# Gate logits of two branches by Strassen's method in a hybrid decoder layer

## The chip, the cores and the metric

The kernel runs on one core of a Trainium2 chip. The metric is the device time of one execution in microseconds, as the median of several runs.

## What is computed

One layer on 1024 tokens of width 1024, all in float32. `x` is multiplied by one wide input projection; three causal token mixers (stick-breaking attention, a gated linear recurrence with 64-wide state (HGRN2), and one with low-rank forget gates (GLA)) give three branches of width 256. Each branch n is projected up to 1024 columns and weighted by a gate of its own, whose logits are 1024 more columns of the input projection:

```python
up = jnp.einsum('nbtw,nwd->nbtd', branches, w_up)
gates = jax.nn.sigmoid(jnp.stack([gate_logits_a, gate_logits_b, gate_logits_c], axis=0))
merged = jnp.sum(gates * up, axis=0)
out = jnp.einsum('btd,de->bte', merged, w_out)
return layer_norm(DEEPNORM_ALPHA * x + out, ln_g, ln_b)
```

The gate logits of one branch are thus a product of a 1024 x 1024 matrix of weights and the transposed x (1024 x 1024).

## The kernel before, in words

**Numbers.** Every float32 operand of a matmul is split into a hi part (rounded, by a ScalarE cast, L98) and a lo part (what is left, by a VectorE subtraction, L99; both in `split`). A product is three matmuls: hi x hi, hi x lo, lo x hi. The transposed x stays in on-chip memory as hi and lo: `xh[th][g]` and `xl[th][g]`, where th is the half of the tokens (512) and g the half of the contraction (four k tiles of 128 rows): eight buffers of the tag `x`.

**Weights.** `load_w` (L167) brings 128 columns of weights in pieces of 256 KB into raw buffers (tag `wr`, four of them, issued by SyncE) and splits them into `wh` and `wl` (five buffers each) at a high priority (`at_priority(PW)`).

**Buffers.** The row buffers (`R`, tag `row`, eight of 128x512), the larger ones (`S`, tag `s`, six of 128x1024), `H` (29 of 128x512), `GT` (two) and the PSUM banks (`pmm` three, `pz` two, `ptr` two, `pav` one) are shared by name: whoever asks for one waits until one is released.

**Order.** The mixers are chains (`c_sb`, `c_rec`) whose steps are interleaved in the code with a stream of projection work, a list of generators (L787 to L792) that give way after every six matmuls of 512 columns or so; `advance` takes the next step of the stream, and entries of `later` are run a counted number of steps on. Once the chains are done, the rest of the stream follows alone: what is left of the gates of branch 0 (`g0`), the finish of branch 1's mixer (`f_finish`), then the gates of branch 2 (`g2`) and branch 1 (`g1`). The instructions of each engine are laid in an order at build time, by priority and by what is ready, and an engine then runs its own list in that order.

**A gate block** (`f_gate`, L488). For each of the eight blocks dd of 128 columns: the weights of the logits (eight k tiles, two loads) and of the up projection (two k tiles, one load) are loaded and split; then for each half of the tokens 24 matmuls of 512 columns (`proj_T`, L207) into a PSUM bank, a sigmoid (L499, ScalarE), six up matmuls (L505) into another bank, the product of the two (L510, VectorE) and an addition to the merged row `mT[dd][th]` (L511, GpSimd).

**The tail** (L855 on). `wout` loads and splits the eight blocks of `w_out`, two of them (`NWO`) ahead of the last gate block into H buffers, the other six into the `x` buffers as these come free. For each quarter of the tokens `mT` is split into `mh` and `ml` (eight row buffers in all); for each 128 tokens 48 matmuls of 512 columns (L879) are followed by the layer norm on VectorE (L881 to L894) in a row `xr` (an S buffer, loaded at L870), which goes out through two DMA queues.

Of the kernel before, what the change touches and what calls it, by code (L numbers as in the profile page):

```python
# [7 lines left out]
F32 = mybir.dt.float32  # L8
F32R = mybir.dt.float32r
# [3 lines left out]
ALU = mybir.AluOpType  # L13
# [17 lines left out]
NGT = 2  # L31
PW = -3000000
PX = -3000000
NWO = 2
NWARM = 10
SB_T = 1.6
CV_T = 10.0
# [18 lines left out]
def hybrid_layer_kernel(ctx, tc, x, x_t, w_in, gla_gate_w2, gla_gate_b, hgrn_lb_logits,  # L56
# [12 lines left out]
    def nm(s):  # L69
        cnt[0] += 1  # L70
        return f"{s}_{cnt[0]}"

    def S(name, dt=F32, shape=None):
        return sp.tile(shape or [P, 1024], dt, tag="s", name=nm(name), bufs=NS)

    def H(name, dt=F32, shape=None):
        return sp.tile(shape or [P, 512], dt, tag="h", name=nm(name), bufs=NH)

    def R(name, dt=F32, shape=None):
        return sp.tile(shape or [P, 512], dt, tag="row", name=nm(name), bufs=NROW)  # L80
# [4 lines left out]
    def pmm(shape=None):  # L85
        return ps.tile(shape or [P, 512], F32, tag="mm", name=nm("mm"), bufs=3)

    def pz(shape=None):
        return ps.tile(shape or [P, 512], F32, tag="z", name=nm("z"), bufs=2)
# [7 lines left out]
    def split(hi, lo, src):  # L97
        nc.scalar.copy(hi, src)  # L98
        nc.vector.tensor_tensor(lo, src, hi.bitcast(F32), op=ALU.subtract)  # L99
# [341 lines left out]
    def f_finish(c0, gain, key, out_key):  # L441

        ws = load_w(W, c0)
        while key not in d:
            yield 0.0
        og, yT = d[key], [[H("yT") for _ in range(2)] for _ in range(2)]

        def transposed(tq):
            for c in range(2):
                pt = ptr([P, 4, P])  # L450
                for t4 in range(4):
                    for o, n, c1 in og(tq * 4 + t4):
                        if c1 <= c * P < c1 + n:
                            nc.tensor.transpose(pt[:, t4, :], o[:, c * P - c1:c * P - c1 + P], ident)
                nc.scalar.copy(yT[c][tq], pt.rearrange("p a b -> p (a b)"))

        for tt in range(8):
            pt = yield from proj_N(ws, tt)
            g = GT("gg")[:, 0:256]
            nc.scalar.activation(g, pt, AF.Sigmoid)  # L460
            nc.vector.tensor_tensor(g, pt, g, op=ALU.mult)
            nc.gpsimd.tensor_tensor(g, g, gain, op=ALU.mult)
            for o, n, c in og(tt):
                nc.vector.tensor_tensor(o, o, g[:, c:c + n], op=ALU.mult)
            yield 1.3
            if tt == 3 + FIN:
                transposed(0)
                yield 0.9

        def rest():  # L470
            transposed(1)
            d[out_key] = yT

        later.append([FIN2, rest])

    def f_split(n):
        while ("y", n) not in d:
            yield 0.0
        r = []
        for c in range(2):  # L480
            yh, yl = [H("yh", F32R) for _ in range(2)], [H("yl", F32R) for _ in range(2)]
            for th in range(2):
                split(yh[th], yl[th], d["y", n][c][th])
            r.append((yh, yl))
        d["ys", n] = r
        yield 0.0

    def f_gate(n, first, d0=0, d1=8):  # L488
        for dd in range(d0, d1):
            if first:  # L490
                d.setdefault("mT", []).append([H("mT") for _ in range(2)])
            ug = load_w(W, GATE0 + 1024 * n + dd * P, P)
            uu = load_w(w_up[0, n], dd * P, P)
            for th in range(2):
                mT = d["mT"][dd][th]
                pt = yield from proj_T(ug, th)
                yield 1.3
                gt = GT("gt")
                nc.scalar.activation(gt, pt, AF.Sigmoid)  # L499
                pu = pmm()  # L500
                k = 0
                for c in range(2):
                    (wh, wl), (a, b) = uu[c], d["ys", n][c]
                    for w_, y_ in ((wh, a), (wh, b), (wl, a)):
                        mm(pu, w_, y_[th], start=(k == 0), stop=(k == 5))  # L505
                        k += 1
                if first:
                    nc.vector.tensor_tensor(mT, pu, gt, op=ALU.mult)  # L508
                else:
                    nc.vector.tensor_tensor(gt, pu, gt, op=ALU.mult)  # L510
                    nc.gpsimd.tensor_tensor(mT, mT, gt, op=ALU.add)  # L511
                yield 1.3

    woh, wol = [], []

    def wout(ks):
        for k in ks:
            if k < NWO:
                wh, wl = [[H("wo", F32R) for _ in range(2)] for _ in range(2)]
            else:  # L520
                w = xp.tile([P, 4, 512], F32R, tag="x", name=nm("wo"))
                wh, wl = [[w[:, 2 * i + e] for e in range(2)] for i in range(2)]
            for e in range(2):
                raw = wp.tile([P, 512], F32, tag="wr", name=nm("wr"), bufs=NWR)
                nc.sync.dma_start(raw, w_out[0, k * P:(k + 1) * P, half[e]])
                with at_priority(PW):
                    split(wh[e], wl[e], raw)
            woh.append(wh)
            wol.append(wl)

    def f_wout(ks):
        wout(ks)
        yield 0.0
# [98 lines left out]
    def c_rec(key, nh, V):  # L632
# [139 lines left out]
        for i, o in enumerate(og):  # L772
# [15 lines left out]
              ("fC", f_cv()), (("ag", 1), f_ag(1)), ("KC", f_ck()), ("GLA", f_cq()),  # L788
              (("ys", 0), f_split(0)), ("g0", f_gate(0, True, 0, 2)), ("vH", f_hi()), (("H", 0), f_h(0)),
              (("y", 2), f_finish(C_G, gng, "ogC", ("y", 2))), (("H", 1), f_h(1)), ("g0", f_gate(0, True, 2, 8)),  # L790
              (("y", 1), f_finish(H_G, hng, "ogH", ("y", 1))), (("ys", 2), f_split(2)), ("g2", f_gate(2, False)),
              (("ys", 1), f_split(1)), ("g1", f_gate(1, False, 0, 7)), ("wo", f_wout(range(NWO))), ("g1", f_gate(1, False, 7, 8))]  # L792
    pos = [0]
    later = []
    budget = [0.0]
# [1 line left out]
    def advance():  # L797

        while pos[0] < len(stream):
            for entry in list(later):  # L800
                entry[0] -= 1
                if entry[0] < 0:
                    later.remove(entry)
                    entry[1]()
            try:
                return next(stream[pos[0]][1])
            except StopIteration:
                done.add(stream[pos[0]][0])
                pos[0] += 1
        return None  # L810
# [26 lines left out]
    for label, mk in chains:  # L837
        need(label)
        for t_fill in mk():
            budget[0] = max(budget[0], -3.0) + t_fill  # L840
            while budget[0] > 0:
                c = advance()
                if c is None or c == 0.0:
                    break
                budget[0] -= c
        if label == "GLA":
            d["ogC"] = og_c
        if label == ("H", 1):
            d["ogH"] = og_h
    while advance() is not None:  # L850
        pass
    mT = d["mT"]
# [94 lines left out]
```

## Time and profile before

| what | value |
|---|---|
| median of 3 runs | 836.09 us (835.85 to 836.49) |
| profiled execution, its own time | 836.32 us |
| its span, first to last instruction | 834.4 us |
| TensorE busy | 814.6 us, 98% |
| VectorE busy | 478.2 us, 57% |
| ScalarE busy | 351.8 us, 42% |
| GpSimd busy | 192.9 us, 23% |

All times of the trace count from the span's first instruction. PE is TensorE's matmul, PEld its loading of weights, DVE VectorE, ACT ScalarE, POOL GpSimd, SP SyncE; L207 is line 207 of the kernel. "[2.37 <-PE mm L207]" behind an instruction says that its engine had been idle for 2.37 us, and what ended that. The ends of matmuls are modelled and overlap the next one's start: the distance of two starts is the time that one takes.

### The profile page before, as it was taken

Reading aid. Unit: us, or ns where it says so; the run is one execution under the profiler, and the core shown is the slowest. Engines: PE = TensorE matmul, PEld = TensorE weight load, DVE = VectorE, ACT = ScalarE, POOL = GpSimd, SP = SyncE. Lnnn points to the kernel's source line nnn. Section 1 sums busy time; section 2 is a strip of 40 time slices with the busy share of each in tenths; the row PEclk is TensorE's granted clock in tenths of the full one; section 3 lists DMA queues with packets and bytes.
Section 4 is the critical chain, followed back from the end, with each engine's and each line's share of the span. In section 5 each row is a group of like instructions: output and inputs, shape, how many; then the busy total and the mean of one; then the engine's idle time right before and its main releaser. Section 6 shows DMA issues by size and latency. Waiting matters only on the chain.

```text
span 834.4 us, 12375 instructions
## 1 busy us (share of the span) xinstructions
PE 814.6 (98%) x4576; PEld 696.6 (83%) x4576; DVE 478.2 (57%) x905; ACT 351.8 (42%) x733; POOL 192.9 (23%) x362
## 2 busy tenths in 40 slices
PE   8999999999899999999999999999999999999996
PEld 7987799787689989988888889888888888888886
DVE  6469998869975578667844224222232223266665
ACT  6466565696544737455545213221222222241110
POOL 3011213131777722221110002222222221210000
PEclk9999999999999999999999999999999999999999
DMA  9421000110010101100412211121212122132211
GB/s 268 111 54 26 26 26 2 45 45 26 13 39 26 52 25 27 45 20 20 133 33 82 64 45 38 43 54 38 57 34 62 35 60 65 43 127 101 101 51 51
DMA packets 66508, 46.22 MB, mean 55 GB/s; under 512 B 4352, under 2 KB 61328, under 8 KB 66448
## 3 DMA queue, kind: packets, MB, share of 16 engines
q1 hardware_dynamic: 65008, 42.36, 18.1%
q10 hardware_dynamic: 1440, 3.08, 1.0%
q8 instruction: 36, 0.59, 0.3%
q14 instruction: 24, 0.20, 0.1%
HBM read 41.23 MB, written 4.19 MB: 54 GB/s over the span
## 4 chain that ended last, share of the span: by engine, by line
PE 87%; DVE 6%; issue 2%; ACT 2%; POOL 1%; DMA 1%; SPq 0%; POOLq 0%; DVEq 0%; ACTq 0%
PE mm L207 43%; PE mm L220 13%; PE mm L879 11%; PE mm L505 8%; PE z L694 5%; PE av L608 2%; PE av L767 2%; DVE om L570 1%; PE tr L586 1%; PE av L765 1%; PE z L745 1%; DVE be L571 1%; DMA xraw<-in_x_t_dram 1%; DVE atl L99 1%; PE z L560 1%
## 5 line engine op out<-in xcount | busy, mean ns | idle before, releaser
L207 PE MATMUL mm<-xh,wh 128*128 128x512 f32 x576 | 231.1, 401 | 0.0
L207 PE MATMUL mm<-xh,wl 128*128 128x512 f32 x576 | 229.5, 398 | 0.0
L207 PE MATMUL mm<-xl,wh 128*128 128x512 f32 x576 | 228.7, 397 | 0.0
L207 PEld LDWEIGHTS mm<-xh,wh 128*128 128x128 f32 x576 | 110.0, 191 | 23.0 <-DVE mT L508 0.2
L207 PEld LDWEIGHTS mm<-xh,wl 128*128 128x128 f32 x576 | 108.7, 189 | 24.2
L207 PEld LDWEIGHTS mm<-xl,wh 128*128 128x128 f32 x576 | 109.0, 189 | 22.6
L99 DVE TENSOR_TENSOR wl<-wr,wh 128x512 fp32r<-128x512 f32 (+2 forms) x116 | 76.0, 661 | 78.6 <-ACT wh L98 76.8
L98 ACT CAST wh<-wr 128x512 fp32r<-128x512 f32 (+2 forms) x116 | 66.4, 576 | 105.2 <-PE mm L207 92.9
L220 PE MATMUL mm<-wh,xh 128*128 128x256 f32 (+1 forms) x320 | 92.0, 287 | 0.5 <-ACT wh L98 0.3
L220 PE MATMUL mm<-wl,xh 128*128 128x256 f32 (+1 forms) x320 | 91.0, 284 | 0.7 <-DVE wl L99 0.7
L220 PE MATMUL mm<-wh,xl 128*128 128x256 f32 (+1 forms) x320 | 90.5, 283 | 0.1
L511 POOL TENSOR_TENSOR mT<-mT,gt 128x512 f32<-128x512 f32 x32 | 46.5, 1453 | 178.4 <-DVE gt L510 178.4
L879 PE MATMUL mm<-wo,mh 128*128 128x512 f32 (+1 forms) x288 | 80.6, 365 | 0.0
L499 ACT ACTIVATE gt<-mm 128x512 f32<-128x512 f32 x48 | 28.6, 595 | 99.7 <-PE mm L207 90.5
L510 DVE TENSOR_TENSOR gt<-mm,gt 128x512 f32<-128x512 f32 x32 | 22.1, 691 | 83.2 <-PE mm L505 82.9
L220 PEld LDWEIGHTS mm<-wh,xh 128*128 128x128 f32 x320 | 60.4, 189 | 1.6 <-ACT wh L98 1.4
L220 PEld LDWEIGHTS mm<-wl,xh 128*128 128x128 f32 x320 | 60.3, 188 | 1.3 <-DVE wl L99 1.3
L220 PEld LDWEIGHTS mm<-wh,xl 128*128 128x128 f32 x320 | 60.4, 189 | 0.4 <-DVE xl L99 0.3
L879 PEld LDWEIGHTS mm<-wo,mh 128*128 128x128 f32 x288 | 52.1, 189 | 8.8
L879 PE MATMUL mm<-wo,ml 128*128 128x512 f32 (+1 forms) x144 | 52.6, 366 | 0.0
L678 POOL TENSOR_TENSOR Qlo<-Q,Qbd 32x128 fp32r<-32x128 f32 x96 | 51.0, 548 | 3.5 <-ACT Qbd L675 0.9
L566 POOL TENSOR_SCALAR_AFFINE_SELECT om<-om 128x128 f32<-128x128 f32 x32 | 12.8, 401 | 141.5 <-ACT om L561 137.9
(204 smaller groups left out, 1334.7 us busy)
## 6 DMA issues: line engine op xcount, KB each, us to landing
wr<-in_w_in_dram SPq DMA_DIRECT2D x92, 256.0 KB, 2.8
xraw<-in_x_t_dram SPq DMA_DIRECT2D x16, 256.0 KB, 5.6
xr<-in_x_dram SPq DMA_DIRECT2D x8, 512.0 KB, 3.2
wr<-in_w_out_dram SPq DMA_DIRECT2D x16, 256.0 KB, 2.8
wr<-in_w_up_dram SPq DMA_DIRECT2D x24, 128.0 KB, 2.2
out_dram<-xr SPq DMA_DIRECT2D x7, 256.0 KB, 2.1
out_dram<-xr ACTq DMA_DIRECT2D x7, 256.0 KB, 2.1
lng<-in_ln_g_dram ACTq DMA_DIRECT2D x1, 512.0 KB, 4.4
```

The lines of the kernel that those rows point to most:

```text
L98: nc.scalar.copy(hi, src)
L99: nc.vector.tensor_tensor(lo, src, hi.bitcast(F32), op=ALU.subtract)
L207: mm(pt, w_, x_, start=(n == 0), stop=(n == 23))
L220: mm(pt, x_, w_, start=(n == 0), stop=(n == 23))
L499: nc.scalar.activation(gt, pt, AF.Sigmoid)
L505: mm(pu, w_, y_[th], start=(k == 0), stop=(k == 5))
L510: nc.vector.tensor_tensor(gt, pu, gt, op=ALU.mult)
L511: nc.gpsimd.tensor_tensor(mT, mT, gt, op=ALU.add)
L608: mm(p_, v, a_[:, s, :], start=(4 * g + ns == nst and s == 0 and n == 0), stop=(g == 0 and s == ns - 1 and n == 1))
L678: nc.gpsimd.tensor_tensor(Qlo[hf][i][rr, a, :].rearrange("p (n h) -> p n h", h=h), qo[rr, i * nb * 2:i * nb * 2 + nb * 2], Qbd[hf].bitcast ...
L694: mm(pt[:, wi * nh:(wi + 1) * nh], k_[:, w * P:(w + 1) * P], q.rearrange("p a (n h) -> p a n h", h=h), start=(n == 0 and wi == 0), stop=(n ...
L879: mm(pt, l_, r_[e][:, o:o + w], start=(n == 0), stop=(n == 23))
```

## The change

`g2` and `g1` no longer go block by block (`f_gate`) but in pairs of blocks (`f_gate2`, four pairs a branch). In a pair, the first three k tiles of each half of the contraction, the two column blocks and the two halves of the tokens form a product of two 2 x 2 matrices of blocks, and this is computed with seven products of sums in place of eight. The fourth k tile of both halves (`rest`) and the up projections stay as they were. The sums of x (T1 to T3, hi and lo: six S and six row buffers, held until the end of `g1`; T4 in place of three k tiles of x) are computed once, in steps put into `later` after the chains; T4 stands in the stream ahead of `g2`. The sums of the weights (S1 to S4) are computed for each pair. The products are kept and added by VectorE and ScalarE. `NWO` is 1, and the second block of `w_out` goes into two S buffers.

```diff
-NWO = 2
+NWO = 1
...
+    NS2 = 3
...
+    def x_sums():
...
+        def make(t, k, terms):
+            f = R("xf")
+            sum_of(f, terms)
+            split(TS[t][0][k], TS[t][1][k], f)
+            return f
+
+        def first(k):
+            (h11, l11), (h12, l12), (h22, l22) = x_part(0, 0, k), x_part(0, 1, k), x_part(1, 1, k)
+            f = make(1, k, [(h12, 1), (h11, -1), (l12, 1), (l11, -1)])
+            make(2, k, [(h22, 1), (f, -1), (l22, 1)])
+
+        def second(k):
+            (h12, l12), (h22, l22) = x_part(0, 1, k), x_part(1, 1, k)
+            make(3, k, [(h22, 1), (h12, -1), (l22, 1), (l12, -1)])
...
+    def f_last_sum():
+
+        TS[4] = [[xx[1][0][:, k] for k in range(NS2)] for xx in (xh, xl)]
+        for k in range(NS2):
+            h21, l21 = x_part(1, 0, k)
+            f = R("xf")
+            sum_of(f, [(h21, 1), (TS[2][0][k].bitcast(F32), -1), (l21, 1), (TS[2][1][k].bitcast(F32), -1)])
+            split(TS[4][0][k], TS[4][1][k], f)
+        yield 0.0
+
+    def f_gate2(n, d0, d1):
+        for dd in range(d0, d1, 2):
...
+            with at_priority(PW):
+                raw(0, 0), raw(1, 0), raw(1, 1), raw(0, 1)
+                a11, a21, a22, a12 = [raws[ij][:, c3] for ij in ((0, 0), (1, 0), (1, 1), (0, 1))]
+                tt_ = nc.vector.tensor_tensor
+                split(*room("A11"), raws[0, 0])
+
+                tt_(a11, a11, a21, op=ALU.subtract)
+                tt_(a21, a21, a22, op=ALU.add)
+                split(*[t[:, c3] for t in room("S1")], a21)
+
+                s2 = H("s2", shape=[P, 4, P])[:, c3]
+                tt_(s2, a22, a11, op=ALU.subtract)
+                split(*[t[:, c3] for t in room("S2")], s2)
+                split(*room("A12"), raws[0, 1])
+                tt_(s2, a12, s2, op=ALU.subtract)
+                up_weights(0)
+                s3 = room("S3")
+                split(*[t[:, c3] for t in s3], a11)
+                split(*[t[:, 3] for t in s3], raws[1, 0][:, 3])
+                split(*room("A22"), raws[1, 1])
+                up_weights(1)
+                split(*[t[:, c3] for t in room("S4")], s2)
...
+            def gated(i, j, z, pu, g):
+
+                nc.scalar.activation(g, z, AF.Sigmoid)
+                nc.vector.tensor_tensor(g, pu, g, op=ALU.mult)
+                mT = d["mT"][dd + i][j]
+                nc.gpsimd.tensor_tensor(mT, mT, g, op=ALU.add)
+
+            bA, bB, bC, bD = pz(), pz(), ptr(), ptr()
+            p1, u2 = R("p1"), R("u2")
+            yield from series(bA, sums("A11", X(0, 0)), True, True)
+            nc.scalar.copy(p1, bA)
...
+            yield from series(bC, sums("S1", TS[1]), True, True)
...
+            yield from series(bB, sums("S2", TS[2]), True, True)
+            nc.vector.tensor_tensor(u2, p1, bB, op=ALU.add)
+            nc.vector.tensor_tensor(u2, u2, bC, op=ALU.add)
...
+            yield from series(bA, sums("A12", X(1, 0)) + rest(0, 0), False, True)
...
+            yield from series(bD, rest(0, 1), True, False)
...
+            pu00 = yield from up(0, 0)
+            gated(0, 0, bA, pu00, GT("gt"))
...
+            pu01 = yield from up(0, 1)
...
+            yield from series(bB, sums("S3", TS[3]), False, True)
+            u3 = GT("u3")
+            nc.vector.tensor_tensor(u3, p1, bB, op=ALU.add)
...
+            yield from series(bB, sums("A22", TS[4]) + rest(1, 0), False, True)
+            nc.vector.tensor_tensor(p1, p1, bB, op=ALU.add)
...
+            yield from series(bC, rest(1, 1), False, True)
+            nc.vector.tensor_tensor(u3, u3, bC, op=ALU.add)
...
+            pu10 = yield from up(1, 0)
+            gated(1, 0, p1, pu10, p1)
...
+            pu11 = yield from up(1, 1)
+            gated(1, 1, u3, pu11, u3)
...
+            yield from series(bD, sums("S4", X(1, 1)), False, True)
+            nc.vector.tensor_tensor(u2, u2, bD, op=ALU.add)
+            gated(0, 1, u2, pu01, u2)
...
+            elif k == NWO:
+                w = [S("wo", F32R, [P, 2, 512]) for _ in range(2)]
...
-              (("y", 1), f_finish(H_G, hng, "ogH", ("y", 1))), (("ys", 2), f_split(2)), ("g2", f_gate(2, False)),
-              (("ys", 1), f_split(1)), ("g1", f_gate(1, False, 0, 7)), ("wo", f_wout(range(NWO))), ("g1", f_gate(1, False, 7, 8))]
+              (("y", 1), f_finish(H_G, hng, "ogH", ("y", 1))), (("ys", 2), f_split(2)), ("T4", f_last_sum()), ("g2", f_gate2(2, 0, 8)),
+              (("ys", 1), f_split(1)), ("g1", f_gate2(1, 0, 6)), ("wo", f_wout(range(NWO))), ("g1", f_gate2(1, 6, 8))]
...
+    for i, step in enumerate(x_sums()):
+        later.append([1 + 3 * i, step])
```

`series` issues the three matmuls of each k tile in order (hi x hi, hi x lo, lo x hi); `X(i, j)` are the first three k tiles of `xh[j][i]` and `xl[j][i]`; `room` asks for one `wh` and one `wl` buffer; `raw` loads one column block of one half of the contraction (256 KB), `up_weights` the up weights of one block (128 KB), which are split into one buffer.

## Rows read from the trace of the kernel before

**Rows 1.** The page: busy us (share of span), instructions; tenths of 40 slices.
```profile
PE 814.6 (98%) x4576; PEld 696.6 (83%) x4576; DVE 478.2 (57%) x905; ACT 351.8 (42%) x733; POOL 192.9 (23%) x362
...
PE   8999999999899999999999999999999999999996
...
PEclk9999999999999999999999999999999999999999
```

**Rows 2.** Chain of waits in order of time, gate stage and tail: start, us, step.
```profile
515.12 5.59 PE mm L207 x24
520.71 1.39 PE mm L505 x6
...
613.63 5.58 PE mm L207 x24
619.21 1.39 PE mm L505 x6
...
737.78 1.39 PE mm L505 x6
739.17 87.70 PE mm L879 x432
```

**Rows 3.** Busy time by stretch: stretch and length, each engine's us, clock, DMA.
```profile
450.00:460.00 10.00, 10.00 (x44) 8.11 (x44) 3.84 (x8) 5.06 (x8) 0.00 (x0) 1.00 0.23 76
460.00:470.00 10.00, 10.00 (x44) 8.11 (x43) 2.15 (x4) 2.34 (x4) 0.00 (x0) 1.00 0.29 80
470.00:480.00 10.00, 10.00 (x44) 8.12 (x43) 2.50 (x4) 2.15 (x4) 0.00 (x0) 1.00 0.21 54
480.00:490.00 10.00, 10.00 (x44) 8.10 (x43) 2.08 (x3) 1.22 (x3) 0.00 (x0) 1.00 0.12 31
490.00:500.00 10.00, 10.00 (x80) 9.71 (x79) 3.82 (x9) 2.50 (x5) 1.48 (x2) 1.00 0.24 61
500.00:515.00 15.00, 15.00 (x130) 15.00 (x129) 7.38 (x20) 6.73 (x14) 3.68 (x5) 1.00 0.01 1
...
627.00:739.00 112.00, 112.00 (x483) 90.87 (x482) 35.16 (x57) 29.65 (x57) 22.85 (x16) 1.00 0.22 64
```

**Rows 4.** Instructions by line and shape, 515.1 to 739.2 us: busy, mean, idle before.
```profile
L511 POOL TENSOR_TENSOR mT<-mT,gt 128x512 f32<-128x512 f32 x31 | 45.2, 1458 | 173.1 <-DVE gt L510 173.1
...
L510 DVE TENSOR_TENSOR gt<-mm,gt 128x512 f32<-128x512 f32 x31 | 21.4, 691 | 83.2 <-PE mm L505 82.9 <-ACT wo L98 0.3
L99 DVE TENSOR_TENSOR wl<-wr,wh 128x512 fp32r<-128x512 f32 x30 | 20.5, 687 | 35.7 <-ACT wh L98 35.7
L499 ACT ACTIVATE gt<-mm 128x512 f32<-128x512 f32 x32 | 19.1, 595 | 77.6 <-PE mm L207 77.6
L98 ACT CAST wh<-wr 128x512 fp32r<-128x512 f32 x29 | 18.0, 620 | 37.1 <-PE mm L207 33.4 <-ACT gt L499 3.1 <-PE mm L505 0.6
...
L99 DVE TENSOR_TENSOR wo<-wr,wo 128x512 fp32r<-128x512 f32 x12 | 9.8, 844 | 4.9 <-ACT wo L98 3.0 <-PE mm L505 1.8
...
L99 DVE TENSOR_TENSOR wl<-wr,wh 128x256 fp32r<-128x256 f32 x16 | 6.8, 425 | 16.7 <-ACT wh L98 16.7
L98 ACT CAST wh<-wr 128x256 fp32r<-128x256 f32 x15 | 6.1, 406 | 21.3 <-PE mm L207 21.3
```

**Rows 5.** Timeline: a hand-over from TensorE to VectorE, and one from VectorE to TensorE.
```profile
703.92 0.40 PE L505 MATMUL mm<-yh,wl 128*128 128x512 f32 x1
...
704.42 0.69 DVE L510 TENSOR_TENSOR gt<-mm,gt 128x512 f32<-128x512 f32 x1 [3.29 <-PE mm L505]
...
302.40 1.10 PE L745 MATMUL z<-vC,kn 128*128 128x256 f32 x4 [0.21 <-DVE St L753]
```

**Rows 6.** Timeline of TensorE, 315 to 319 us, in a chain's stretch.
```profile
315.48 0.40 PE L207 MATMUL mm<-xl,wh 128*128 128x512 f32 x1
315.71 0.59 PE L765 MATMUL av<-St,Q 128*128 128x256 f32 x2
316.14 1.00 PE L767 MATMUL av<-vC,sc 128*128 128x64 f32 x8
316.98 0.65 PE L765 MATMUL av<-St,Q 128*128 128x256 f32 x2
317.47 1.00 PE L767 MATMUL av<-vC,sc 128*128 128x64 f32 x8
318.28 0.47 PE L207 MATMUL mm<-xh,wl 128*128 128x512 f32 x1
```

**Rows 7.** Timeline of ScalarE: a merged row of the tail is cast in the gate stage.
```profile
650.77 0.41 ACT L98 CAST mh<-mT 128x256 fp32r<-128x256 f32 x1 [3.03 <-POOL mT L511]
```

**Rows 8.** Timeline, end of the gates and begin of the tail (739 us).
```profile
727.80 1.14 ACT L98 CAST wo<-wr 128x512 fp32r<-128x512 f32 x2 [3.35 <-PE mm L207]
...
735.00 1.30 POOL L511 TENSOR_TENSOR mT<-mT,gt 128x512 f32<-128x512 f32 x1 [7.54 <-DVE gt L510]
...
742.69 0.62 ACT L98 CAST wo<-wr 128x512 fp32r<-128x512 f32 x1 [0.44 <-DMA wr<-in_w_out_dram]
```

**Rows 9.** Chain of waits up to 745 us: the first matmuls of the tail.
```profile
739.17 5.91 PE mm L879 x26
```

**Rows 10.** Timeline of the first x row of the tail; the page's DMA times to landing.
```profile
754.83 0.35 ACTq L895 DMA_DIRECT2D out_dram<-xr  x1
...
xr<-in_x_dram SPq DMA_DIRECT2D x8, 512.0 KB, 3.2
...
out_dram<-xr ACTq DMA_DIRECT2D x7, 256.0 KB, 2.1
```

**Rows 11.** Who waited for whom, 440 to 745 us: total, times, longest.
```profile
ACT wh L98 <- PE mm L207: 76.5, 28, 4.8
```

More of the change, by code (lines that the diff above doesn't have):

```diff
@@ L512, in f_gate, with x_part, sum_of, room @@
                 yield 1.3
+    NS2 = 3
+    def x_part(i, j, k):
+        return xh[j][i].bitcast(F32)[:, k], xl[j][i].bitcast(F32)[:, k]
+    def sum_of(dst, terms):
+        (a, _), (b, sb) = terms[:2]
+        nc.vector.tensor_tensor(dst, a, b, op=ALU.add if sb > 0 else ALU.subtract)
+        for c, sc_ in terms[2:]:
+            nc.vector.tensor_tensor(dst, dst, c, op=ALU.add if sc_ > 0 else ALU.subtract)
+    TS = {}
+    def x_sums():
+        def room():
+            for t in (1, 2, 3):
+                a = [S("xs", F32R, [P, 2, 512]) for _ in range(2)]
+                b = [R("xs", F32R) for _ in range(2)]
+                TS[t] = [[a[e][:, 0], a[e][:, 1], b[e]] for e in range(2)]
+        def make(t, k, terms):
[10 more added lines that the diff above has]
+            make(3, k, [(h22, 1), (h12, -1), (l22, 1), (l12, -1)])
+        steps = [room]
+        for k in range(NS2):
+            steps += [lambda k=k: first(k), lambda k=k: second(k)]
+        return steps
@@ L519, in wout @@
                 wh, wl = [[H("wo", F32R) for _ in range(2)] for _ in range(2)]
+            elif k == NWO:
+                w = [S("wo", F32R, [P, 2, 512]) for _ in range(2)]
+                wh, wl = [[t[:, e] for e in range(2)] for t in w]
             else:
```

54 lines of the change are left out of this document (added).

## The prediction
> **What bounds the kernel now.** I read the page first. TensorE is busy for 98% of the span, and its granted clock is in the top tenth in all 40 slices; the next engine, VectorE, is busy for 57% [rows 1]. A busy matmul row is no proof of a bound, because matmuls overlap, so I went on to the chain of waits: from 515 us to 827 us it is TensorE alone, each step following the one before without a gap [rows 2]. The gate stage of branches 2 and 1 runs from 515.12 to 739.17 us: 32 times (two branches, eight blocks, two halves of the tokens) a step of 24 gate matmuls (5.58 us) and 6 up matmuls (1.39 us). The tail, 432 matmuls, follows at once. So in this stretch a matmul less is its pitch less, as long as nothing makes TensorE wait: 5.585/24 = 0.2327 us. The other engines have room there: in 627 to 739 us VectorE is busy for 35 us of 112 and ScalarE for 30 [rows 3].
>
> **What is removed.** For a pair of column blocks the old code issues 2 x 2 x 30 = 120 matmuls. The new one has seven products of nine (three k tiles, three hi/lo terms each), 63; the fourth k tile of both triples stays as it was, four blocks of six, 24; the up projections are four of six, 24. That is 111. Nine less per pair, eight pairs, 72 in all, at 0.2327 us: **16.75 us less**. The 256 KB and 128 KB loads stay the same in number. The Trainium skill, "TensorE: Matmul & The Clock Gate", section "Wait — 56ns, not 53.3ns?", gives 215.7 ns from start to start for 512 columns; by it the term would be 15.5 us. The trace differs, and the measurement decides. The sum goes by 0.2327.
>
> **What is added in a pair.** A pair should last 111 x 0.2327 = 25.8 us. VectorE takes 0.69 us for 512 columns and 0.43 for 256 [rows 4]; for 384 I estimate 0.56, half way. Ten subtractions for the hi/lo splits: 3 x 0.69 + 4 x 0.56 + 0.3 + 2 x 0.43 = 5.5 us; four sums of weight blocks, 2.2; six sums that read a product from PSUM, priced as the gate's product with a PSUM operand, 0.69 each [rows 4], 4.1; four gate products, 2.8. Together 14.6 us of 25.8, where it was 6.4 of 27.9. ScalarE has about 8.0 us (casts 5.0, four sigmoids at 0.60, one PSUM copy at 0.6), GpSimd 4 x 1.46 = 5.8 as before. None of them becomes the bound by its sum; what can cost is who waits for whom.
>
> The buffers: eight hi tiles and eight lo tiles per pair go through five buffers each. Counted in matmuls of a pair, S1's and S2's come free at 18 and 27, A11's and A12's at 48, S3's and A22's at 90, S4's at 111. The tightest claim is the lo part of the next S1, which takes a buffer free at 90 and is read at 120: 30 x 0.233 = 7.0 us for a cast and a subtraction of about 1.1 us. I cost it at nothing; what hides it are the up matmuls and S4. The two row buffers for the kept product and for the sum u2 are renewed each pair: u2's is free some 4 us after S4, its next writer runs 27 matmuls (6.3 us) after S4. Nothing again.
>
> One wait is new. Product S3 and then product A22 accumulate in the same PSUM bank, and between them VectorE must read it (u3). A hand-over of this kind shows in rows: VectorE starts 0.50 us after the start of the last matmul and takes 0.69, and a matmul that waited for VectorE idled for 0.21 [rows 5]. That is 1.40 us from start to start in place of 0.23: 1.17 us lost, eight times, 9.4 us, the upper end. The lower end is nothing: the six matmuls of the next accumulation but one, rest(1,1), lie in another bank, need nothing of u3 and fill 1.4 us. The order on TensorE in this program is not the order of the code: a run of projection matmuls is interrupted between the second and the third matmul of one k tile, where the code never gives way (it does so after every sixth), and the third follows behind twenty of another chain [rows 6]. So the order is laid by what is ready, and I take 0.1 us each, **0.8 us**.
>
> **What is added outside.** The sums of x are 33 VectorE instructions of 512 columns (24 sums, 9 subtractions), 22.8 us, and 9 casts, issued from about 452 us on. VectorE is busy for 22 us in the 65 from 450 to 515 [rows 3], so they fit; a step of eight can hold up a gate product for 5.5 us, and a third PSUM buffer covers about 6. The last sum, 12 instructions, 8.3 us, is due 69 matmuls (16 us) into the first pair, beside that pair's own splits. For both I take **0.7 us**, between nothing and 2.
>
> **The tail.** Before, the casts and subtractions of the merged rows were done as each gate block ended, some 90 us ahead [rows 7], into eight row buffers. Now six of these hold sums of x and two the kept sums, so the last one comes free after S4, by u2's sum 0.69, sigmoid 0.60, product 0.69, GpSimd 1.30 [rows 8] and four hand-overs of 0.1 to 0.2: 3.9 us; with a subtraction of 0.43 the rows of k = 6 are whole at 4.3, and the tail wants them after 19 matmuls at 5.91/26 = 0.227 us [rows 9], 4.3. The weights of the tail are late too: x tiles come free 27 matmuls (6.3 us) before the end, the first w_out cast before was 11.4 us ahead of it [rows 8]. VectorE has 11 splits (0.69 to 0.84), three or four sums and products and the last rows to do in some 11 us: 11 x 0.69 + 4 x 0.69 + 1.7 = 12 us. Ends: nothing, if other columns of the tail are put ahead; 5 us, if not. I take **1.0**, near the lower end, because the order by readiness [rows 6] applies here as well. One block of w_out less is loaded early (NWO); its two casts fall into the last pair, where ScalarE has room. The x rows of the tail have two buffers in place of four: a row is out 0.3 us after 754.8 plus 2.1, its reload is 3.2 us [rows 10], so it lands near 761 and is wanted at about 767. Nothing.
>
> **The sum.** 16.75 - 0.8 - 0.7 - 1.0 = 14.25 us less. All of it lies inside the profiled span (834.4 us; the execution took 836.32, the 1.9 around stay). That execution is 0.23 above the median, 836.09; from the median I get 821.8.
>
> **The rivals.** *The wait on u3 is not filled.* For it: the code writes A22 straight behind the read. The Trainium skill, same page, section "The mechanism" of Part 3, says that matmuls start in strict program order, so that the chip itself fills nothing; [rows 6] concern the order in the program and do not contradict it. Against it: the same rows, and that no step of the stage has an idle stretch before it now [rows 2]. Time: 836.1 - 16.75 + 9.4 + 1.7 = 830.4. *The tail starts late*, by the full 5 us: 836.1 - 16.75 + 0.8 + 0.7 + 5.0 = 825.8. For it the row buffers above; against it, that all work up to k = 5 can run. *Both, with the ends of the rest:* 836.1 - 16.75 + 9.4 + 5 + 1.5 = 835.2, no change to be seen. *The weights of a product come late*, the one that ends slower. Its place is the start of a product. ScalarE already waits for TensorE's release of a weight buffer [rows 11], and if the splits of S1 to S4 are queued behind work that waits for PSUM, they start only as the product before ends: cast, subtraction and the hand-over, 0.5 + 0.56 + 0.3, about 1.4 us. At two of seven products per pair that is 16 x 1.4 = 22.4 us: 836.1 - 16.75 + 22.4 + 1.7 = 843.4. It decides from 15/1.4 = 11 late products of 56. Against it the 7 us of the tightest claim.
>
> **How the numbers follow.** Forecast 0.62 (819.3 to 825), tail late 0.13, u3 unfilled 0.13, both 0.05, weights late 0.07. Range 818.8 to 831: its low end is the 16.75 without any wait and half a microsecond for the pitch, its high end u3 unfilled. A measurement of this kernel tells 0.2%, 1.7 us, from no change: faster is 0.62 + 0.13 + 0.13 = 0.88, same 0.05, slower 0.07.
>
> **What would show it.** The gate stage of branches 2 and 1 should last 8 x 25.8 = 207 us, 888 matmuls, with VectorE at 55 to 60%. Right or wrong of the u3 step: what stands on TensorE between S3 and A22, rest(1,1) or a gap of 1.2 us that ends with a VectorE read. Of the tail: idle time ahead of the first 24 tail matmuls, ended by the last rows or by w_out. Of the weights: TensorE idle at the first matmul of a product, ended by a cast or a split. A stage of 207 us with the end still at 834 would mean that the tail took it back; a stage above 222 us, that the change fails where it acts.

## The result, and the profile after

The changed kernel takes **824.26 us** (median of 4 runs, 822.14 to 825.62); the kernel before, run beside it, 835.97 (4 runs). The ratio is 0.9857, 95% interval [0.9842, 0.9872]: 11.7 us less. The profiled execution of after took 824.63 us, its span is 822.6, against 836.32 and 834.4 before. The forecast was 821.8, the range 818.8 to 831.0. Two executions among the runs below, one of e2_late (2690.94 us) and one of e9_raws_ml (875.17 us), were in a slow state; the medians given count them, the ratios leave them out.

In the page of the kernel after, TensorE is still the busiest engine, VectorE went from 57% [rows 1] to 71%.

```profile
PE 800.5 (97%) x4504; PEld 683.8 (83%) x4504; DVE 583.5 (71%) x1062; ACT 374.5 (46%) x785; POOL 191.7 (23%) x362
```

The busy time by stretch splits the span at 722.50, where the last gate matmul gives way to the first of the tail (columns as in [rows 3]).

```profile
514.50:722.50 208.00, 207.89 (x899) 167.41 (x898) 139.01 (x215) 70.30 (x141) 42.29 (x31) 1.00 0.25 71
722.50:822.60 100.10, 89.66 (x433) 75.61 (x431) 64.52 (x129) 16.16 (x42) 4.85 (x5) 0.97 0.24 84
728.00:730.00 2.00, 0.00 (x0) 0.00 (x0) 2.00 (x3) 1.37 (x3) 1.58 (x1) 1.00 0.06 22
730.00:732.00 2.00, 1.23 (x3) 1.03 (x4) 1.66 (x4) 0.94 (x1) 0.00 (x0) 0.67 0.00 0
732.00:734.00 2.00, 2.00 (x6) 1.52 (x6) 0.26 (x1) 0.00 (x0) 0.00 (x0) 0.50 0.00 0
```

For the kernel before, here are the busy time of its tail and the first matmul of its gate stage:

```profile
739.00:834.40 95.40, 87.86 (x433) 74.52 (x431) 59.91 (x123) 14.51 (x38) 2.79 (x3) 0.98 0.21 75
...
514.95 0.40 PE L207 MATMUL mm<-xh,wh 128*128 128x512 f32 x1
```

So the gate stage of branches 2 and 1 lasts 722.50 - 514.54 = 208.0 us (its first matmul starts at 514.54) where it lasted 739.00 - 514.95 = 224.05: **16.1 us less**. It starts 0.4 us earlier. The tail lasts 100.1 us where it lasted 95.4: **4.7 us more**. 16.1 + 0.4 - 4.7 = 11.8, the difference of the spans. Of the 16.75 us that were forecast for the nine matmuls, 16.1 are there, and the tail took back more than a quarter of that. (The times are those of the profiled executions; the four executions of after differ by up to 3.5 us.)

The chain of waits of the kernel after shows both. A pair of column blocks is 710.76 - 684.95 = 25.81 us, TensorE all through (the 0.93 us between the first two lines are four matmuls of another accumulation, shown next for another pair). Then, at the tail, VectorE's splits of w_out stand in the chain, where [rows 2] had TensorE alone.

```profile
684.95 2.10 PE z L622 x9
687.98 3.59 PE z L622 x15
...
710.76 2.08 PE z L622 x9
...
724.35 1.78 DVE wo L99
728.03 1.87 DVE wo L99 x2
730.77 84.31 PE mm L1062 x409
```

**Inside a pair.** TensorE's timeline where product S3 (`z<-xs`) ends and A22 (`z<-xh`) begins, in the same bank:

```profile
557.42 0.40 PE L622 MATMUL z<-xs,wl 128*128 128x512 f32 x1
557.65 0.39 PE L622 MATMUL tr<-xh,wh 128*128 128x512 f32 x1
...
558.34 0.40 PE L622 MATMUL tr<-xh,wh 128*128 128x512 f32 x1
558.59 0.50 PE L622 MATMUL z<-xh,wh 128*128 128x512 f32 x1
558.93 0.39 PE L622 MATMUL z<-xl,wh 128*128 128x512 f32 x1
...
562.17 0.39 PE L622 MATMUL tr<-xl,wh 128*128 128x512 f32 x1
```

VectorE's timeline, with its read of that bank:

```profile
557.85 0.69 DVE L673 TENSOR_TENSOR u<-p,z 128x512 f32<-128x512 f32 x1 [0.44 <-PE z L622]
```

Four of the six matmuls of `rest(1,1)` were put into the wait, and the last two follow after A22 and `rest(1,0)`, from 562.17. They cover the read but for a remainder: it ends at 558.54, A22 starts at 558.59, and its second matmul follows 0.34 us later. From 557.42 to 558.93 the six starts take 1.51 us instead of 6 x 0.232 = 1.39, 0.12 us more. The same stands at all eight hand-overs, 0.11 to 0.14 us each, 1.0 us in all.

**At the tail.** TensorE's timeline:

```profile
722.26 0.40 PE L622 MATMUL tr<-xh,wl 128*128 128x512 f32 x1
722.50 0.39 PE L1062 MATMUL mm<-wo,mh 128*128 128x512 f32 x1
...
727.26 0.61 PE L1062 MATMUL mm<-wo,mh 128*128 128x512 f32 x2
730.77 0.79 PE L1062 MATMUL mm<-wo,ml 128*128 128x512 f32 x1 [2.90 <-DVE ml L99]
731.37 1.05 PE L1062 MATMUL mm<-wo,mh 128*128 128x512 f32 x2
732.22 1.05 PE L1062 MATMUL mm<-wo,ml 128*128 128x512 f32 x2
733.07 1.34 PE L1062 MATMUL mm<-wo,mh 128*128 128x512 f32 x3
734.25 0.40 PE L1062 MATMUL mm<-wo,ml 128*128 128x512 f32 x1
```

After 23 matmuls of the tail it waits for a lo row of the merged output. At the pitch of 0.227 us the next matmul would have started at 727.49 + 0.23 = 727.72; it starts at 730.77, 3.05 us late. The eight matmuls from there to 734.25 take 3.48 us instead of 8 x 0.227 = 1.82, 1.66 us more: the granted clock in the table above fell from 1.00 to 0.50, the 1.2 GHz level, behind the idle stretch. 3.05 + 1.66 = 4.7 us: that is the whole loss of the tail.

What the row waited for stands in the timeline of VectorE and GpSimd in the same stretch (L647 is a gate's product, L649 GpSimd's addition to mT, L688 the last sum u2, `wo<-wr,wo` the splits of w_out):

```profile
721.07 1.60 POOL L649 TENSOR_TENSOR mT<-mT,p 128x512 f32<-128x512 f32 x1 [9.39 <-DVE p L647]
723.97 1.60 POOL L649 TENSOR_TENSOR mT<-mT,u 128x512 f32<-128x512 f32 x1 [1.29 <-DVE u L647]
728.26 1.58 POOL L649 TENSOR_TENSOR mT<-mT,u 128x512 f32<-128x512 f32 x1 [2.68 <-DVE u L647]
...
720.84 2.38 DVE L99 TENSOR_TENSOR wo<-wr,wo 128x512 fp32r<-128x512 f32 x2
...
723.75 2.37 DVE L99 TENSOR_TENSOR wo<-wr,wo 128x512 fp32r<-128x512 f32 x2
726.05 0.67 DVE L688 TENSOR_TENSOR u<-u,tr 128x512 f32<-128x512 f32 x1
...
727.42 0.69 DVE L647 TENSOR_TENSOR u<-mm,u 128x512 f32<-128x512 f32 x1
728.03 2.36 DVE L99 TENSOR_TENSOR wo<-wr,wo 128x512 fp32r<-128x512 f32 x2
730.31 0.41 DVE L99 TENSOR_TENSOR ml<-mT,mh 128x256 fp32r<-128x256 f32 x1
```

Two splits take 2.36 to 2.38 us when a GpSimd addition runs beside them, three times over; two splits with nothing beside them take 1.29 us (in the kernel before):

```profile
728.45 1.29 DVE L99 TENSOR_TENSOR wo<-wr,wo 128x512 fp32r<-128x512 f32 x2 [2.43 <-ACT wo L98]
```

The sum u2 could start at 722.26 + 0.50 = 722.76 (the last matmul of S4 and the hand-over of [rows 5]) and starts at 726.05, behind stretched splits; the row that TensorE wants is split at 730.31, behind the third stretched pair. Two readings are open from here: the row buffer that u2 holds comes free late, or VectorE itself is behind.

### The profile page after: what moved, and what is told of

It is laid out like the page before. It is cut to its first block, busy times and chain, and to the rows that moved or that the text cites. A ratio compares the mean times of both kernels' runs of the same rounds, so it can differ in the third digit from the quotient of the medians.

```text
span 822.6 us, 12504 instructions
## 1 busy us (share of the span) xinstructions
PE 800.5 (97%) x4504; PEld 683.8 (83%) x4504; DVE 583.5 (71%) x1062; ACT 374.5 (46%) x785; POOL 191.7 (23%) x362
## 4 chain that ended last, share of the span: by engine, by line
PE 85%; DVE 7%; issue 3%; ACT 2%; DMA 1%; POOL 1%; POOLq 0%; SPq 0%; DVEq 0%; ACTq 0%
PE mm L207 22%; PE mm L220 14%; PE z L622 12%; PE mm L1062 10%; PE tr L622 6%; PE mm L622 5%; PE z L875 5%; PE mm L505 3%; PE av L789 2%; PE av L948 2%; DVE om L751 1%; PE tr L767 1%; PE av L946 1%; PE z L926 1%; DVE be L752 1%
## 5 line engine op out<-in xcount | busy, mean ns | idle before, releaser
L207 PE MATMUL mm<-xh,wh 128*128 128x512 f32 x320 | 130.6, 408 | 0.0
L207 PE MATMUL mm<-xh,wl 128*128 128x512 f32 x320 | 127.5, 398 | 0.0
L207 PE MATMUL mm<-xl,wh 128*128 128x512 f32 x320 | 127.0, 397 | 0.0
L99 DVE TENSOR_TENSOR wl<-wr,wh 128x512 fp32r<-128x512 f32 (+3 forms) x116 | 80.3, 701 | 48.6 <-PE z L622 22.5
L98 ACT CAST wh<-wr 128x512 fp32r<-128x512 f32 (+3 forms) x116 | 64.6, 569 | 78.0 <-PE mm L207 32.9
L207 PEld LDWEIGHTS mm<-xh,wl 128*128 128x128 f32 x320 | 60.5, 189 | 13.5
L207 PEld LDWEIGHTS mm<-xh,wh 128*128 128x128 f32 x320 | 61.0, 191 | 11.8 <-DVE mT L508 0.4
L207 PEld LDWEIGHTS mm<-xl,wh 128*128 128x128 f32 x320 | 60.8, 190 | 11.2
L622 PE MATMUL mm<-yh,wu 128*128 128x512 f32 x128 | 42.4, 392 | 0.0
L622 PE MATMUL z<-xh,wh 128*128 128x512 f32 x104 | 41.6, 400 | 0.0
```

The source lines that it names most:

```text
L207: mm(pt, w_, x_, start=(n == 0), stop=(n == 23))
L622: mm(pt, w_, x_, start=(start and i == 0), stop=(stop and i == len(ops) - 1), skip_group_check=True)
```

## The experiments

All are edits of the kernel after, except the two controls, which are edits of the kernel before. "The first theory" is the row buffers, "the rival" late w_out blocks; a third, VectorE's own load, came up on the way.

**e1_ml: another buffer for the last lo rows.**

```diff
-        ml = [R("ml", F32R, [P, 2, 256]) for _ in range(4)]
+        ml = [R("ml", F32R, [P, 2, 256]) for _ in range(3)]
+        ml.append(wp.tile([P, 2, 256], F32R, tag="wl", name=nm("ml"), bufs=5))
```

> The lo rows of k = 6 and 7 take a weight buffer in place of a row buffer, so they no longer wait for u2's buffer. Theory rows (the tail waits for u2's row buffer): TensorE's 2.9 us of idle time ahead of the 23rd tail matmul fall to under 0.5, the clock stays up, the span falls by about 4.5 us, from 822.6 to 818. Rival weights (the splits of the last w_out block end at 730.39 us anyway, 3 us late): idle time of 2 to 3 us stays, now ended by a w_out split, and the span stays within 1 us of 822.6.

823.24 us, ratio to before 0.9852 [0.9838, 0.9867]. TensorE's timeline still shows a wait for the lo row, half as long:

```profile
731.18 0.50 PE L1063 MATMUL mm<-wo,ml 128*128 128x512 f32 x1 [1.43 <-DVE ml L99]
```

The buffer is part of that wait, not the whole; the time itself is not told apart from after's (0.9857 [0.9842, 0.9872]). A second finding: the granted clock is 1.00 in 730 to 734 us here, so after 1.43 us of waiting there was no drop. The busy time of the second half of that stretch:

```profile
732.00:734.00 2.00, 2.00 (x10) 1.67 (x9) 1.33 (x2) 0.00 (x0) 0.00 (x0) 1.00 0.00 0
```

**e2_late: e1_ml, and in the last pair the last two gated products at the lowest priority**, so that the splits of w_out are laid ahead of them.

```diff
+            with at_priority(PLATE if n == 1 and dd == 6 else 0):
+                gated(1, 1, u3, pu11, u3)
...
+            with at_priority(PLATE if n == 1 and dd == 6 else 0):
+                nc.vector.tensor_tensor(u2, u2, bD, op=ALU.add)
+                gated(0, 1, u2, pu01, u2)
```

> As e1_ml, and in the last pair the gates of the second half of the tokens, which the tail wants only 45 us later, get the lowest priority. Theory rows: no better than e1_ml. Rival weights: VectorE and ScalarE reach the last w_out splits some 1.4 to 2.4 us earlier, since a sum and a product (0.69 each) and the stretch under GpSimd's addition lie ahead of them now; the idle time falls to about 1 us, the span by 2 to 4 us against the changed kernel.

822.96 us, 0.9849 [0.9829, 0.9868]: with e1_ml's 0.9852, no difference that shows. TensorE now waits twice, 1.1 us together, for splits of w_out. The idle time is the one that the rival expected, about 1 us, but of the 2 to 4 us that it promised, 3.2 show in the profiled execution (span 819.4) and only 1.3 in the median: another order shortens the wait a little and moves it from the lo rows to the splits.

**e4_order: the matmuls of the new gate stage held in the order of the code.** This tests the other uncertain step, the wait on u3.

```diff
-                    mm(pt, w_, x_, start=..., stop=...)
+                    with tc.issue_after(prev[0]) if prev else nullcontext():
+                        r = mm(pt, w_, x_, start=..., stop=...)
+                    prev[:] = [getattr(r, "ins", r)]
```

> TensorE issues all matmuls of the pairs in the order of the code, so nothing fills the wait between S3 and A22. Theory fill (the four matmuls of rest(1,1) that stand there now hide the whole wait): a gap of 1.0 to 1.2 us in each of the eight pairs, a pair of 27.0 us in place of 25.85, the span longer by 8 to 9.5 us, about 831. Rival (the read of the bank takes no time that TensorE feels): gaps under 0.3 us and a span within 2 us of 822.6.

One execution: 831.5 us, span 829.8. Who waited for whom (total, times, longest), and two starts of the same product in the chain of waits:

```profile
PE z L625 <- DVE u L677: 7.0, 8, 0.9
```

```profile
582.52 2.10 PE z L625 x9
...
609.32 2.10 PE z L625 x9
```

A pair is 609.32 - 582.52 = 26.80 us, 1.0 more than in after; TensorE idles for 0.9 us at the read of u3 in each of the eight pairs when nothing fills it. The 2.9 us at the tail stay. So it was the order laid at build time that made this wait free. The Trainium skill, "TensorE: Matmul & The Clock Gate", section "The mechanism" of Part 3, says that matmuls start strictly in program order. This run agrees: TensorE idles 0.9 us eight times although `rest(1,1)`, which needs nothing of u3, stands next in its list behind A22.

**e6_nwo: the kernel before with one block of w_out less ahead of the last gate block** (`NWO = 1`, the second block in two S buffers), the part of the change that touches the tail's weights.

> The kernel before, with the one part of the change that concerns w_out: one block loaded early, the second in two S buffers, so that the x rows of the tail have two buffers. Theory rows: nothing to see, a span of 834 to 835, because the row buffers are free here. Rival weights: one block less ahead makes the last w_out split 1.3 us later, 0.5 to 2 us of idle time on TensorE within the first 24 tail matmuls, a span of 835 to 837.

One execution: 836.42 us, span 834.4 as before. In the kernel before, that part alone costs nothing.

**e9_raws_ml and e11_raws: the last raw w_out tiles in the weight buffers**, so that their loads need not wait for a raw buffer; the first with e1_ml's buffer, the second without.

```diff
-                raw = wp.tile([P, 512], F32, tag="wr", ..., bufs=NWR)
+                raw = wp.tile(..., tag="wr", ..., bufs=NWR) if k < 5 else wp.tile(..., tag=("wh", "wl")[e], ..., bufs=5)
```

> The changed kernel with the lo rows of k = 6 and 7 in a weight buffer (as e1_ml) and the raw tiles of the last three w_out blocks in wh and wl buffers, which are free by then, so that these blocks are loaded ahead of the end of the gates. Theory both (the tail waits for u2's row buffer and, just as late, for the last w_out split): with both waits gone TensorE idles for under 0.6 us ahead of the first 24 tail matmuls, the clock stays up, span 818 to 819, median 820. Theory rows alone: no better than e1_ml, 820.8 span, 823.2 median. A third, VectorE's own load: idle time of 1 to 2 us stays, ended by an ml subtraction that stands behind the w_out splits.

> Only the raw tiles of the last three w_out blocks in wh and wl buffers; the lo rows still wait for u2's row buffer. Theory both: the idle time ahead of the tail's last rows stays at 2 to 3 us, ended by ml, since u2's sum and product now stand behind more splits; span within 1 us of 822.6. Theory weights alone: it falls to under 0.6, span 818 to 819.

822.6 us (0.9838 [0.9825, 0.985]) and 821.58 us (0.9832 [0.982, 0.9845]); the two are not told apart. In each two waits of 0.75 to 0.83 us are left in place of one of 2.9, in e11_raws without the extra buffer too. Neither number expected for e11_raws came out: one theory let 2 to 3 us stay, the other under 0.6. In e9_raws_ml, the 1.6 us left are what the expectation named for VectorE's own load. VectorE's timeline of e9_raws_ml shows why the waits got shorter: eight splits stand in one row now and meet one addition of GpSimd, which begins at 722.02, instead of three.

```profile
722.38 5.70 DVE L99 TENSOR_TENSOR wo<-wr,wo 128x512 fp32r<-128x512 f32 x8 [0.51 <-ACT wo L98]
```

That made VectorE's speed itself the suspect.

**e5_dveall: every addition to mT in the new stage on VectorE**, GpSimd idle there; e12_dveall5 is the same kernel, timed four times.

```diff
-                nc.gpsimd.tensor_tensor(mT, mT, g, op=ALU.add)
+                nc.vector.tensor_tensor(mT, mT, g, op=ALU.add)
```

> All additions to mT in the gates of branches 2 and 1 on VectorE, GpSimd idle there. Theory contention: the 512-column splits of the weights, 0.946 us in the mean in the seven steady pairs, fall to 0.69, and the up weights' from 0.877 to 0.43; VectorE is busy for 14.6 + 4 x 0.7 = 17.4 us a pair, where it was 16.4 to 17.9; a pair stays at 25.85. Rival: the means stay, VectorE at 19.5 us or more a pair.

> The same kernel as e5_dveall, timed: all additions to mT in the gates of branches 2 and 1 on VectorE. Theory contention (the tail was late because three of GpSimd's additions stretch VectorE's splits there): the tail starts without a wait of TensorE, span near 817.5, median 819 to 820, faster than the changed kernel by 4 to 5 us.

819.49 us in one execution, then 820.32 (819.45 to 820.76), ratio 0.9815 [0.9802, 0.9829]. No wait of TensorE is left in the tail. VectorE does 27 instructions more in 529.7 to 710.6 us and is busy for less: 118.34 us in after, 115.48 here. The groups by shape of that stretch, first in after, then in e5_dveall, show what became faster:

```profile
L99 DVE TENSOR_TENSOR wl<-wr,wh 128x512 fp32r<-128x512 f32 x20 | 18.9, 946 | 4.2 <-PE mm L622 2.4 <-ACT wh L98 1.7
...
L601 DVE TENSOR_TENSOR s<-wr,wr 128x384 f32<-128x384 f32 x7 | 10.5, 1494 | 0.0
L647 DVE TENSOR_TENSOR u<-mm,u 128x512 f32<-128x512 f32 x14 | 9.6, 685 | 4.6 <-ACT u L646 4.5
```

```profile
L99 DVE TENSOR_TENSOR wl<-wr,wh 128x512 fp32r<-128x512 f32 x20 | 13.7, 687 | 2.2 <-ACT wh L98 2.2
L647 DVE TENSOR_TENSOR u<-mm,u 128x512 f32<-128x512 f32 x14 | 9.6, 687 | 4.2 <-ACT u L646 4.2
...
L601 DVE TENSOR_TENSOR s<-wr,wr 128x384 f32<-128x384 f32 x6 | 3.3, 550 | 0.0
```

Subtractions with both operands in SBUF go from 946 to 687 ns and from 1494 to 550; the product with an operand in PSUM takes 685 and 687.

**e8_dveadd: e9_raws_ml with e2_late's priorities, and the last pair's additions on VectorE.**

> As e9_raws_ml, and in the last pair the gates of the second half of the tokens at the lowest priority and the additions to mT on VectorE in place of GpSimd. Theory contention (a VectorE instruction with two operands in on-chip memory stretches by about 1 us while GpSimd adds): the splits of the last w_out blocks take 0.69 each and none 1.5 or more after 713 us; the tail starts without a wait, span 817.5 to 818.5. Rival (the long splits are long for another reason, such as their raw tiles): splits of 1.5 us remain, and the span is that of e9_raws_ml or longer, by the three additions of 0.69.

821.1 us, 0.9823 [0.9811, 0.9836]; the eight splits take 4.91 us instead of 5.70, and one wait of 0.54 us, for a cast, is left.

**e13_lastdve: the additions on VectorE in the last pair alone**, on the kernel after with nothing else.

```diff
-                nc.gpsimd.tensor_tensor(mT, mT, g, op=ALU.add)
+                eng = nc.vector if n == 1 and dd == 6 else nc.gpsimd
+                eng.tensor_tensor(mT, mT, g, op=ALU.add)
```

> The additions to mT on VectorE in the last pair alone; the other seven pairs keep GpSimd. Theory contention, with its place in the tail alone: span and median as e12_dveall5, 817.5 and 819 to 820, and the long splits stay in the steady pairs at no cost. Rival (the stretch matters in the steady pairs too): 1 us or more longer than e12_dveall5, with TensorE's waits inside the pairs.

**820.11 us** (819.49 to 820.55), 0.9814 [0.9801, 0.9828], the lowest median of all, though not told apart from e12_dveall5. Its tail, from its first matmul at 721.6:

```profile
721.60:817.50 95.90, 88.14 (x433) 74.44 (x431) 63.59 (x131) 16.61 (x43) 1.50 (x2) 0.98 0.25 88
```

95.9 us, half a microsecond from the 95.4 before, though its pairs ahead keep the stretched splits (948 ns). So the stretch costs time only in the last pair. But the edit also shortens the chain of u2 (no hand-over to GpSimd) and lets the build lay another order of the tail's matmuls. The last run separates these.

**e14_before_dve: the same move of the additions in the kernel before**, as a control.

> Control: the kernel before, with the additions of the gates of branches 2 and 1 on VectorE. Theory contention: no change, 835.5 to 836.5, since TensorE does not wait in the old gate stage and tail. Rival (GpSimd's additions cost time of their own at the end): 1 us or more faster.

835.47 us, ratio 1.0 [0.9991, 1.0009]. The splits of w_out do become faster there, 690 ns where [rows 4] have 844, and nobody waits for them:

```profile
L99 DVE TENSOR_TENSOR wo<-wr,wo 128x512 fp32r<-128x512 f32 x12 | 8.0, 690 | 4.9 <-ACT wo L98 3.0 <-PE mm L505 1.8
```

**e15_memset: GpSimd keeps its place in the chain, but only writes.** This kernel leaves out the sum over the branches for the last two column blocks: their merged rows are zero.

```diff
-                nc.gpsimd.tensor_tensor(mT, mT, g, op=ALU.add)
+                if n == 1 and dd == 6:
+                    r = nc.gpsimd.memset(g, 0.0)
+                    with tc.issue_after(getattr(r, "ins", r)):
+                        nc.gpsimd.memset(mT, 0.0)
+                else:
+                    nc.gpsimd.tensor_tensor(mT, mT, g, op=ALU.add)
```

> The kernel after, in which GpSimd's four additions to mT in the last pair of column blocks are each replaced by two memsets of GpSimd, one of the gated tile and one of mT behind it (128x512 each; such a memset takes 0.52 us elsewhere in the trace, so 1.05 us for the two against 1.29 us for an addition that meets nothing and 1.58 to 1.60 us for one that meets VectorE). So the third triple's sum for the last two column blocks is left out and mT[6] and mT[7] are zero there. Every engine keeps the order of its instructions, VectorE and TensorE alike, and the hand-over VectorE, GpSimd, ScalarE, VectorE stays; only GpSimd's reading of SBUF is gone. Theory (contention: VectorE's subtractions are stretched while GpSimd adds): the pairs of w_out splits take 1.29 instead of 2.37 us, three stretches of 1.05 us go, the first tail matmul with ml comes by 728 instead of 730.8, no idle stretch over 1 us is left and the granted clock stays at 1.00; 819.5 to 821 us in the mean, span 817.5 to 819. Rival (the length of the chain through GpSimd and the order of instructions, not the contention): the chain is shorter by 0.2 to 0.5 us for each hand-over only, an idle stretch of 2 to 2.7 us stays, 823.5 to 824.5 us.

820.57 us (820.12 to 821.47), 0.9823 [0.9806, 0.9839], span 818.7. The order of the instructions on VectorE and on TensorE is that of after. Timeline of GpSimd, VectorE and TensorE:

```profile
722.59 0.53 POOL L650 MEMSET u<- 128x512 f32 x1 [1.08 <-DVE u L647]
723.05 0.53 POOL L652 MEMSET mT<- 128x512 f32 x1
...
722.38 1.28 DVE L99 TENSOR_TENSOR wo<-wr,wo 128x512 fp32r<-128x512 f32 x2
723.59 0.68 DVE L693 TENSOR_TENSOR u<-u,tr 128x512 f32<-128x512 f32 x1
...
725.11 0.68 DVE L647 TENSOR_TENSOR u<-mm,u 128x512 f32<-128x512 f32 x1
...
727.81 0.42 DVE L99 TENSOR_TENSOR ml<-mT,mh 128x256 fp32r<-128x256 f32 x1
...
728.28 0.51 PE L1067 MATMUL mm<-wo,ml 128*128 128x512 f32 x1 [0.94 <-DVE ml L99]
```

The splits beside GpSimd's work take 1.28 us, not 2.37. The tail runs from 721.97 to 818.7, 96.7 us: 3.4 of the 4.7 are gone with the order unchanged, and the clock stays at 1.00 in 728 to 732 us. The shorter chain has a share in it, and it is small: a link of GpSimd lasts 0.99 us (722.59 to 723.58) instead of 1.6. Measured from the first matmul of the tail, u2's product starts at 3.14 us (725.11 - 721.97) and in after at 4.92 (727.42 - 722.50): 1.78 us gained ahead of the last link of GpSimd, of 1.97 in all at the lo row (5.84 against 7.81). The theory of contention holds: the tail starts late mainly because GpSimd's additions stretch VectorE's splits. Of the 1.3 us that are still lost, 0.94 are this wait for the lo row. Its buffer is free when GpSimd's last memset ends, at 726.91; its split stands in VectorE's list behind one of w_out (727.20), whose cast had waited 0.92 us for a load. So a late w_out block has a share in what is left.

## Why the prediction was right, and where it was wrong

The time lies in the range, and in the band of the main forecast (819.3 to 825). That it stayed in the band is partly luck: in the trace the rival *the tail starts late* is what happened, and terms that came out lower than taken made up for a part of it.

**The nine matmuls less per pair (16.75 us): right.** A pair lasts 25.81 us where 25.8 was forecast, the stage 208.0 where 207 was. The gain of the stage is 16.1 us, because the hand-overs of u3 take back 1.0; a slightly shorter pitch (0.2319 us in the mean in place of 0.2325) returns some of that.

**The wait on u3 (0.8 us, ends 0 and 9.4): right, in its size too.** It is filled but for 0.12 us a pair, 1.0 us in all, where 0.1 a pair was taken. The reason given, an order laid by readiness, was the right one: with the order of the code a pair is 1.0 us longer (e4_order). That this kernel's 831.5 us is near the rival's 830.4 is partly chance: its eight waits cost 8 us, not 9.4, and its tail loses more than the rival's sum has.

**The sums of x and the last sum (0.7 us): nothing to be seen.** The stage starts at 514.54 against 514.95. In the other kernels, where nothing ahead of it is edited, it starts between 513.5 and 515.5, so that the 0.4 us is no effect either way.

**Weights of a product late (the rival on the slower side): did not happen.** No wait of TensorE in the stage ends with a cast or a split, in spite of splits that are longer than forecast: VectorE is busy for 139 of the 208 us, 67%, where 55 to 60% were expected, and still has room.

**The tail (1.0 us taken, ends 0 and 5): this is the step that failed, in its size; it cost 4.7.** The text took the value "near the lower end, because the order by readiness [rows 6] applies here as well". The order did apply: 23 matmuls run ahead of the wait, 19 were counted on. What failed is the other side, the time when the row is ready. Two sums in it were short:
- The splits were priced "11 x 0.69 + 4 x 0.69 + 1.7 = 12 us". Three additions of GpSimd add 1.07 to 1.09 us each (2.36 to 2.38 against 1.29), 3.2 us. The row that said so was quoted: w_out splits take 844 ns in the mean in [rows 4], and subtractions of the same shape for `wl` 687. The range "0.69 to 0.84" was written down and its lower end multiplied.
- The chain of u2 was started at the end of S4, 3.9 us long. It is 3.8 us long (726.05 to 729.84), but it starts 3.3 us late, because u2's sum stands in VectorE's list behind the stretched splits. Without the stretch (e15_memset) it still starts 723.59 - (721.73 + 0.50) = 1.36 us late, so that 1.4 us are its place in the list and 1.9 the stretch. A chain needs its place in the queue of each engine as well as its durations.

To the 3.05 us that TensorE then waits come 1.66 us at the low level of the clock, for which the prediction has no term; its upper end of 5 us was wide enough all the same. So the tail cost 3.7 us more than was taken. The stage and its start gave 16.1 + 0.4 = 16.5 us, where 16.75 - 0.8 - 0.7 = 15.25 had been counted, 1.25 us better. The difference is the 2.5 us by which the result lies above the forecast; it is nearer to the rival *the tail starts late* (825.8).

**What the change gains when this is mended:** moving four additions of the last pair from GpSimd to VectorE (e13_lastdve) gives 820.11 us, 4.1 less than the kernel after and 15.6 less than the kernel before beside it (835.73). What is left open is how much of that gain over e15_memset's tail (95.9 against 96.7 us) is the missing hand-over and how much the other order of the tail's matmuls.

## What to carry to other kernels

When a change moves work onto a queue that had room, price the queue at the moment of the hand-over to the next stage, with each instruction's place in it, and not the sum over the stage: here VectorE had a third of the stage free, and the time was lost in the ten microseconds around the hand-over. When the same operation with the same shape has two means in the trace (687 and 844 ns), find out what ran beside the longer ones before taking either. The cover of a wait by other work holds in the order in which the engine's list was laid, so read that order, or force the other one, before the wait is costed.

## What was not expected of the hardware

**GpSimd's additions stretch VectorE's subtractions.** A 128x512 subtraction with both operands in SBUF takes 687 ns alone; while GpSimd adds two SBUF tiles, a pair takes 2.37 us instead of 1.29, and GpSimd's addition 1.6 instead of 1.3. Of a pair it is the second split that is stretched, to 1.78 us; the first, which began before the addition, keeps its 0.68. With an operand in PSUM VectorE keeps its 685 ns (the two that ran beside an addition for most of their time in after, at 541.87 and 617.29 us, took 686 and 692), and beside GpSimd's memsets the splits keep theirs (1.28 us the pair). Without GpSimd's additions the groups of the gate stage fall back to 687 and 550 ns. The Trainium skill, "SBUF — State Buffer", section "Who interferes with whom", states this rule: an instruction of VectorE with two SBUF inputs contends with one of GpSimd that reads SBUF, not with one that only writes, and one with at most one SBUF input doesn't, outside VectorE's 2-port modes. The runs agree in all three points; the price, 1.07 to 1.09 us for each addition that ran beside a pair of splits, is this case's.

**The clock behind a short wait.** After 2.90 us without a matmul the granted clock was at 0.50 (1.2 GHz) in 732 to 734 us, which cost 1.66 us on top; after 1.43 us without one (e1_ml) it was at 1.00 (2.4 GHz) in the same stretch.
